# Attention's products with the values as three rounded passes, and the compressed branch as one pass over stacked rows

## The chip, the cores and the metric

The kernel runs on one core of one Trainium2 chip. The metric is the time of the program on the device in microseconds (us), as the median of several runs. TensorE (PE) does the matmuls, VectorE (DVE), ScalarE (ACT) and GpSimd (POOL) the rest, and SyncE (SP) issues the loads. Each of these engines takes its own instructions in turn, and semaphores make one wait for another.

## The reference

One decoder layer: a half-step SwiGLU block, a mixing block with sparse attention and retention side by side, an output projection, and a second half-step SwiGLU block, over 256 positions of width 2048 in float32. What the change touches is the attention, 16 heads of 128 in four groups that share keys and values. Each group has three branches, whose outputs are weighted by gates and added:

```
p_c = masked_softmax(s_c, mask)            # compressed: 15 keys, one per window of 32 positions
o_cmp = einsum('bghsc,bgcd->bsghd', p_c, v_cmp)
o_slc = einsum('bghqnr,bgqnrd->bqghd', p, vg)      # selected blocks (here: all of them)
o_win = einsum('bghnqk,bnkgd->bnqghd', p_w, vw)    # sliding window (here: all of it)
o = gates[:, :, 0] * o_cmp + gates[:, :, 1] * o_slc + gates[:, :, 2] * o_win
```

With 256 positions the selected and the window branch both reduce to causal attention over all keys, each with keys and values of its own.

## The kernel before

**Weights.** Nearly all time goes to products of activations with weights. The weights stream from memory in pieces of 256 rows by 512 columns. `prep` splits each piece (`split`, L134 to L136): ACT rounds it to fp32r (`whi`, L135) and DVE takes the rest (`wlo`, L136). `unit` (L210 to L217) then does one piece as 12 matmuls of 512 columns: high by high, high by low, low by high. One such piece is called a slot here. Up to four pieces are prepared ahead (`PREP`, `AHEAD`). The moving operand of these matmuls is read "by turns" (`by_turns`): one element of the first half, one of the second, and so on; `halves` undoes that where the result is read.

**Order.** The program fixes the order of every engine's instructions by hand (`manual_schedule`). Work that isn't a weight product is cut into small steps that wait in a list (`micro`). `run` takes the weight pieces in order and, after each one, takes one step from the list, so that a step's instructions stand on each engine between those of two slots. Within a step they are issued in the order in which its functions are called.

**Attention.** `attention(g)` projects keys and values of group g (8 slots, `kv_done` at the end), then queries (8 slots, `q_done` at the end). `q_done` adds the group's steps to the list; they are taken one by one during the next 16 slots, under the next group's projections. With the first counted as step 0, the steps are: `k_tr`, two empty ones, `q_tr`, `c_scores` (compressed branch), `scores(1, 1)`, and so on to step 8, `scores(1, 0)` with `scores(0, 0)`, which is taken behind the slot that ends the next group's keys and values and so behind its `kv_done`. Steps 9 to 14 are

```
both(p_tr(1, 1), softmax(1, 0), softmax(0, 0)), p_tr(0, 1), both(pv(1, (1,), False), c_tr),
both(pv(1, (0,), True), p_tr(1, 0), p_tr(0, 0)), None, pv(0, (1, 0), True)]
```

The arguments are branch and half of the queries (`pv`: half, branches, whether the compressed branch is added). `softmax` takes exponentials on ACT (L1004, four of them, each with a sum that is read out), makes weights of the sums on DVE (L931, L932) and POOL, and scales on POOL. `p_tr` transposes the probabilities on PE (L1016), 128 keys at a time, and copies them out of the bank on ACT (first 128 keys, L1021) or DVE (second, L1019). `pv` multiplies values and transposed probabilities in plain float32 (L1033), adds the compressed branch (L1037, 15 rows), and rounds and splits the sum on ACT and DVE (L1044, L1045). `c_tr` transposes the compressed branch's probabilities, 8 blocks of 15 columns (L973), and copies them on ACT (L974).

**Beginning of the mixing block.** `norm` prepares the first half of the positions (`at_once`), the first two slots run on it, and `head` then prepares the second half: DVE scales (L491), ACT rounds (L494), DVE takes the rest (L497). `mix` is the list of all items of the mixing block.

Of the kernel before, what the change touches and what calls it, by code (L numbers as in the profile page):

```python
# [72 lines left out]
def block_kernel(ctx: ExitStack, tc: tile.TileContext, I, konst, decay, out):  # L73
# [714 lines left out]
        return o  # L788

    kcT = cp.tile([P, GROUPS * NCMP], F32, name="kcT")  # L790
    vc = cp.tile([P, GROUPS, DH], F32, name="vc")

    def compress(i):
        def done(ps):
            z = evac(ps)
            box = {}

            def tr():
                zT = t4([P, 4, S])
                banks = to_banks(lambda t, k: z[:, t, k * P:(k + 1) * P])  # L800
                for b in range(2):
                    nc.vector.tensor_copy(zT[:, 2 * b:2 * b + 2], banks[b])
                zp = []
                for h in range(2):
                    zz = t4([P, GROUPS, NCMP, 16])
                    src = bass.AP(tensor=zT.tensor, offset=zT.offset + 16 * h,
                                  ap=[list(zT.ap[0]), [S, GROUPS], [16, NCMP], [1, 16]])
                    pb = pos[:, i, 16 * h:16 * h + 16][:, None, None, :].to_broadcast([P, GROUPS, NCMP, 16])
                    nc.vector.tensor_tensor(zz, src, pb, op=ALU.add)
                    zp.append(zz)  # L810
                box["zp"] = zp

            def first_layer(b):
                def f():
                    if b == 0:
                        box["ps"] = mx()
                    for jj in range(8):
                        j = 8 * b + jj
                        nc.tensor.matmul(box["ps"][:, :60], w1[i][b][:, jj, :],
                                         box["zp"][j // 16][:, :, :, j % 16], start=j == 0, stop=j == 31)  # L820
                    if b == 3:
                        g = small(60, "g60")
                        nc.scalar.activation(g, box["ps"][:, :60], AF.Gelu_apprx_tanh, bias=b1[:, i:i + 1])
                        box["g"] = g
                return f

            def second_layer():
                g = box["g"]
                ps2 = mx()
                if i == 1:  # L830
                    for k in range(GROUPS):
                        nc.tensor.matmul(ps2[0:NCMP, k * DH:(k + 1) * DH], g[:, k * NCMP:(k + 1) * NCMP],
                                         w2[:, 1, :], start=True, stop=True)
                    nc.vector.tensor_copy(vc[0:NCMP], ps2[0:NCMP, :].rearrange("p (g d) -> p g d", g=GROUPS))
                    return
                nc.tensor.matmul(ps2[0:60, :DH], g, w2[:, 0, :], start=True, stop=True)
                kn = t2([P, DH])
                junk = t2([P, DH])
                sc = small(1, "s1")
# [12 lines left out]
            push(tr, None, *[first_layer(b) for b in range(4)], None, second_layer)  # L852
            if i == 0:
                push(None, to_kcT)
        return done

    def gate_logits(hi, lo):
# [14 lines left out]
            nc.vector.tensor_copy(gates, ps[:, :96].rearrange("p (t c) -> p t c", t=2))  # L872
        push(tr)

    mix += in_chunk(O_KV, NCH, compress(0), head)
    mix += in_chunk(O_KV + NCH, NCH, compress(1))
    mix.append(("w", rows(win, 0, KT, O_GL, 48), KT, 48, gate_logits))
# [12 lines left out]
    def attention(g):  # L890
# [1 line left out]
        B3 = [P, 4, DH]  # L892

        def kv_done(ps):
            kv = evac(ps)
            box["kv"] = kv
            for t in range(2):
                ks = [kv[:, t, s * DH:(s + 1) * DH] for s in (0, 2)]
                sc = normed(ks, 2)
                for i, k in enumerate(ks):  # L900
                    nc.gpsimd.tensor_scalar(k, k, sc[:, i:i + 1], None, op0=ALU.mult)

        def q_done(ps):
            q = evac(ps)
# [4 lines left out]
            push(*steps)  # L909

        def k_tr():
            kv = box["kv"]
            kT = t2([P, 2, S])
            ps = mx([P, 2, S])
            for i in range(2):
                for t in range(2):
                    nc.tensor.transpose(ps[:, i, t * P:(t + 1) * P], kv[:, t, 2 * i * DH:(2 * i + 1) * DH], ident)
            for i in range(2):
                nc.scalar.activation(kT[:, i], ps[:, i], AF.Copy, scale=g_qk[:, 2 + i:3 + i])
            box["kT"] = kT  # L920
# [14 lines left out]
        def c_scores():  # L935
            qT = box["qT"]
            ps = mx()
            for t in range(2):
                for h in range(4):
                    c0 = (t * 4 + h) * NCMP  # L940
                    nc.tensor.matmul(ps[:, c0:c0 + NCMP], qT[:, h, t * P:(t + 1) * P],
                                     kcT[:, g * NCMP:(g + 1) * NCMP], start=True, stop=True)
            n = 8 * NCMP
            pc = small(n, "pc")
            pv = pc.rearrange("p (t h c) -> p t h c", t=2, h=4)
            p3 = pc.rearrange("p (a c) -> p a c", c=NCMP)
            nc.vector.tensor_tensor(pv, ps[:, :n].rearrange("p (t h c) -> p t h c", t=2, h=4),
                                    bias_c[:, :, 4 * g:4 * g + 4, :], op=ALU.add)
            m = small(8, "m8")
            nc.vector.tensor_reduce(m, p3, axis=AX.X, op=ALU.max)  # L950
            nc.vector.tensor_tensor(p3, p3, m[:, :, None].to_broadcast([P, 8, NCMP]), op=ALU.subtract)
            box["pc"] = pc

        def c_softmax():
# [9 lines left out]
            weigh(p3, sv, gates[:, :, 4 * g:4 * g + 4], 8)  # L964
            nc.gpsimd.tensor_tensor(p3, p3, s8[:, :, None].to_broadcast([P, 8, NCMP]), op=ALU.mult)

        def c_tr():
            pT = t4([P, 2, NCH])
            for t in range(2):
                ps = mx()  # L970
                for h in range(4):
                    c0 = (t * 4 + h) * NCMP
                    nc.tensor.transpose(ps[0:NCMP, h * P:(h + 1) * P], box["pc"][:, c0:c0 + NCMP], ident)  # L973
                nc.scalar.activation(pT[0:NCMP, t], ps[0:NCMP], AF.Copy)  # L974
            box["pcT"] = pT

        def scores(br, t):
# [32 lines left out]
        def p_tr(br, t):  # L1010
            def f():
                s = box["p", br, t]
                for j in range(t + 1):
                    ps = mx([P, 4, P])
                    for h in range(4):
                        nc.tensor.transpose(ps[:, h], s[:, h, j * P:(j + 1) * P], ident)  # L1016
                    pT = t2([P, 4, P])
                    if j:
                        nc.vector.tensor_copy(pT, ps)  # L1019
                    else:  # L1020
                        nc.scalar.activation(pT, ps, AF.Copy)  # L1021
                    box["pT", br, t, j] = pT
            return f

        def pv(t, brs, cmp_):
            def f():
# [3 lines left out]
                ps = box["o", t]  # L1030
                for br in brs:
                    for j in range(t + 1):
                        nc.tensor.matmul(ps, box["kv"][:, j, (2 * br + 1) * DH:(2 * br + 2) * DH],  # L1033
                                         box["pT", br, t, j].rearrange("p h q -> p (h q)"), start=start, stop=False)
                        start = False
                if cmp_:
                    nc.tensor.matmul(ps, vc[0:NCMP, g, :], box["pcT"][0:NCMP, t], start=False, stop=True)  # L1037
                    if t:
                        o_hi.append(act_hi())
                        o_lo.append(act_lo())  # L1040
                    hi = o_hi[g][:, :, t * P:(t + 1) * P]
                    lo = o_lo[g][:, :, t * P:(t + 1) * P]
                    pq = ps.rearrange("p (h q) -> p h q", h=4)
                    nc.scalar.activation(hi, pq, AF.Copy)  # L1044
                    nc.vector.tensor_tensor(lo, pq, hi.bitcast(F32), op=ALU.subtract)  # L1045
            return f
# [1 line left out]
        def both(*fns):  # L1048
            return lambda: [f() for f in fns]
        steps = [k_tr, None, None, q_tr, c_scores, scores(1, 1), both(softmax(1, 1), scores(0, 1)),  # L1050
                 both(softmax(0, 1), c_softmax), both(scores(1, 0), scores(0, 0)),
                 both(p_tr(1, 1), softmax(1, 0), softmax(0, 0)), p_tr(0, 1), both(pv(1, (1,), False), c_tr),
                 both(pv(1, (0,), True), p_tr(1, 0), p_tr(0, 0)), None, pv(0, (1, 0), True)]
        return (seg_chunk(O_KV + 1024, NCH, 4, g, DH, kv_done)
                + in_chunk(g * NCH, NCH, q_done))
# [193 lines left out]
```

## Time and profile before

| | before |
|---|---|
| median of 3 runs | 2503.43 us (2503.11 to 2505.05) |
| the profiled execution | 2505.49 us, of which its span is 2503.7 us |
| PE busy | 2445.5 us (98%) |
| DVE, ACT, POOL busy | 1737.4 us (69%), 1140.9 us (46%), 233.5 us (9%) |
| the four groups' attention steps | from 890 to 1131 us |

The page of the profile counts an engine busy while it executes an instruction. The timeline lists instructions by engine with start and length. PE's matmuls overlap in it, so that what one costs is the distance between two starts, not its listed length. A float32 matmul shows as two instructions. An idle time and what ended it stand in brackets behind a row.

### The profile page before, as it was taken

The page shows a single profiled execution, that of the slowest core. Times are in us where ns is not written, and L with a number is a line of the kernel's source. Part 1 is how long each engine was busy: PE and PEld are TensorE (multiplying, and loading weights), DVE is VectorE, ACT ScalarE, POOL GpSimd, SP SyncE. Part 2 cuts the span into 40 slices and gives each one's busy share as a digit, 9 for nine tenths or more (in the row PEclk, how much of TensorE's full clock was granted, in tenths as well). Part 3 has the DMA queues.
Part 4 walks back from the last instruction along what each step waited for, and adds up shares of the span by engine and source line. Part 5 has one row for each costly group of instructions (what it writes and reads, how often), then busy time and mean ns, then how long its engine had stood idle before and what let it go on. Part 6 is the DMA issues. An engine that isn't in the chain of part 4 may idle for free. (4 is left out here: it accounts for less than half of the span.)

```text
span 2503.7 us, 31546 instructions
## 1 busy us (share of the span) xinstructions
PE 2445.5 (98%) x11616; PEld 2120.0 (85%) x11616; DVE 1737.4 (69%) x1968; ACT 1140.9 (46%) x1416; POOL 233.5 (9%) x201
## 2 busy tenths in 40 slices
PE   4999999999999999999999999999999999999999
PEld 4888888888887888888888888888788888888888
DVE  7898777898756466776767777776688555555555
ACT  3545444444445355554444444444544444444443
POOL 0000000110002133320000000001100010001001
PEclk9999999999999999999999999999999999999999
DMA  9998888899866455667888877887499666666664
GB/s 347 350 321 277 280 301 293 305 311 344 280 222 196 140 158 143 185 195 261 280 264 262 256 246 235 294 273 250 153 320 352 198 203 199 200 199 203 200 202 153
DMA packets 348339, 616.64 MB, mean 246 GB/s; under 512 B 22044, under 2 KB 80018, under 8 KB 347928
## 3 DMA queue, kind: packets, MB, share of 16 engines
q1 hardware_dynamic: 348184, 614.63, 74.8%
q8 instruction: 91, 1.49, 0.2%
q14 instruction: 64, 0.52, 0.1%
HBM read 612.45 MB, written 2.10 MB: 245 GB/s over the span
## 5 line engine op out<-in xcount | busy, mean ns | idle before, releaser
L136 DVE TENSOR_TENSOR wlo<-raw,whi 128x1024 fp32r<-128x1024 f32 (+1 forms) x865 | 1082.1, 1260 | 575.4 <-ACT whi L135 570.4
L135 ACT ACTIVATE whi<-raw 128x1024 fp32r<-128x1024 f32 (+1 forms) x865 | 906.9, 1056 | 1002.2 <-PE accb L217 730.6
L215 PE MATMUL accb<-whi,ahi 128*128 128x512 f32 x3232 | 1240.5, 384 | 6.1 <-ACT ahi L494 4.7
L216 PE MATMUL accb<-wlo,ahi 128*128 128x512 f32 x3232 | 1229.4, 380 | 3.8 <-DVE wlo L136 3.5
L217 PE MATMUL accb<-whi,alo 128*128 128x512 f32 x3232 | 1228.4, 380 | 2.9 <-DVE alo L541 1.5
L215 PEld LDWEIGHTS accb<-whi,ahi 128*128 128x128 f32 x3232 | 612.8, 190 | 95.1 <-ACT ahi L494 5.5
L216 PEld LDWEIGHTS accb<-wlo,ahi 128*128 128x128 f32 x3232 | 613.0, 190 | 92.2 <-DVE wlo L136 8.0
L217 PEld LDWEIGHTS accb<-whi,alo 128*128 128x128 f32 x3232 | 612.7, 190 | 92.5 <-DVE alo L541 1.9
L344 DVE SCALAR_TENSOR_TENSOR aacc<-raw,cond,aacc 128x1024 f32<-128x1024 f32 x270 | 354.2, 1312 | 1.3 <-DMA raw<-in_w_ada_dram 0.6
L558 POOL TENSOR_TENSOR x<-x,t 128x512 f32<-128x512 f32 x50 | 80.9, 1639 | 1156.2 <-DVE t L556 989.0
L621 PE MATMUL accb<-wlo,ahi 128*128 128x512 f32 x224 | 87.1, 389 | 2.5 <-DVE wlo L136 2.5
L620 PE MATMUL accb<-whi,ahi 128*128 128x512 f32 x224 | 86.7, 387 | 0.0
L622 PE MATMUL accb<-whi,alo 128*128 128x512 f32 x224 | 85.9, 384 | 0.0
L621 PEld LDWEIGHTS accb<-wlo,ahi 128*128 128x128 f32 x224 | 43.0, 192 | 12.1 <-DVE wlo L136 6.2
L540 ACT ACTIVATE ahi<-mx 128x512 fp32r<-128x512 f32 x52 | 28.1, 593 | 53.9 <-PE mx L449 53.9
L541 DVE TENSOR_TENSOR alo<-mx,ahi 128x512 fp32r<-128x512 f32 x52 | 33.4, 684 | 27.2 <-ACT ahi L540 27.2
L620 PEld LDWEIGHTS accb<-whi,ahi 128*128 128x128 f32 x224 | 43.1, 192 | 6.1
L622 PEld LDWEIGHTS accb<-whi,alo 128*128 128x128 f32 x224 | 43.0, 192 | 6.0
L556 DVE TENSOR_TENSOR t<-accb,gt 128x512 f32<-128x512 f32 x56 | 36.3, 683 | 7.7 <-PE accb L217 7.6
L787 ACT ACTIVATE t<-accb 128x512 f32<-128x512 f32 x52 | 30.1, 593 | 24.2 <-PE accb L217 24.1
L1004 ACT ACTIVATE t<-t,m 128x256 f32<-128x256 f32 (+1 forms) x64 | 28.3, 443 | 26.0 <-DVE m L994 26.0
L1113 POOL TENSOR_SCALAR rs<-bmv 128x2 f32<-128x2 f32 x8 | 1.8, 220 | 395.3 <-DVE bmv L1112 395.2
(182 smaller groups left out, 1025.6 us busy)
## 6 DMA issues: line engine op xcount, KB each, us to landing
raw<-in_w_ada_dram SPq DMA_DIRECT2D x288, 512.0 KB, 5.5
raw<-in_w_ffn_gate_dram SPq DMA_DIRECT2D x176, 512.0 KB, 5.1
raw<-in_w_ffn_up_dram SPq DMA_DIRECT2D x176, 512.0 KB, 4.7
raw<-in_w_ffn_down_dram SPq DMA_DIRECT2D x176, 512.0 KB, 4.2
raw<-in_w_in_dram SPq DMA_DIRECT2D x176, 512.0 KB, 4.5
raw<-in_w_in_dram SPq DMA_DIRECT2D x128, 256.0 KB, 3.9
raw<-in_w_proj_nsa_dram SPq DMA_DIRECT2D x32, 512.0 KB, 5.7
raw<-in_w_proj_ret_dram SPq DMA_DIRECT2D x32, 512.0 KB, 5.4
```

What stands on the lines that cost most here:

```text
L135: nc.scalar.activation(hi_ap, raw_ap, AF.Copy)
L136: nc.vector.tensor_tensor(lo_ap, raw_ap, hi_ap.bitcast(F32), op=ALU.subtract)
L215: nc.tensor.matmul(ps[t], xh, wh, start=kt == 0, stop=False)
L216: nc.tensor.matmul(ps[t], xh, wl, start=False, stop=False)
L217: nc.tensor.matmul(ps[t], xl, wh, start=False, stop=kt == K - 1)
L344: nc.vector.scalar_tensor_tensor(box[0], raw, k, box[0], op0=ALU.mult, op1=ALU.add)
L541: nc.vector.tensor_tensor(lo[:, 2 * b:2 * b + 2], ps, h.bitcast(F32), op=ALU.subtract)
L556: nc.vector.tensor_tensor(in_two(y), halves(ps[t]), in_two(gt[:, n * NCH:(n + 1) * NCH]), op=ALU.mult)
L558: (nc.vector if last and n == 3 else nc.gpsimd).tensor_tensor(xs, xs, y, op=ALU.add)
L620: nc.tensor.matmul(ps, xh, h, start=i == 0, stop=False)
L621: nc.tensor.matmul(ps, xh, l, start=False, stop=False)
L622: nc.tensor.matmul(ps, xl, h, start=False, stop=i == nk - 1)
```

## The change

Values and transposed probabilities are now each split into a rounded high part and a low rest, as weights are, and each product is made of three fp32r passes, read by turns. `kv_done` writes keys and values to tiles of their own, the values in two parts. `p_tr` makes both parts of every bank (ACT the high one, DVE the low one). For the compressed branch the probabilities' high part, again the high part and the low part stand at columns 0, 32 and 64 of a zeroed tile `pc3`, and the values' high, low and high part at the same rows of `vc`, so that one fp32r pass over 79 rows gives the three products; a new function `c_split` fills `pc3`, and `clear` zeroes both tiles at the beginning of the mixing block. The list of steps is reordered and has 16 entries. The reading of the result undoes the turns.

```diff
+    CMP = 64 + NCMP
+    vc = cp.tile([P, GROUPS, DH], F32R, name="vc")
+    pc3 = cp.tile([P, 8, CMP], F32R, name="pc3")
+    def clear():
+        nc.scalar.activation(vc, ones[:, None, :].to_broadcast([P, GROUPS, DH]), AF.Copy, scale=0.0)
+        nc.scalar.activation(pc3, ones[:, None, :CMP].to_broadcast([P, 8, CMP]), AF.Copy, scale=0.0)
...
-                    nc.vector.tensor_copy(vc[0:NCMP], ps2[0:NCMP, :].rearrange("p (g d) -> p g d", g=GROUPS))
+                    v = ps2[0:NCMP, :].rearrange("p (g d) -> p g d", g=GROUPS)
+                    for r in (0, 64):
+                        nc.scalar.activation(vc[r:r + NCMP], v, AF.Copy)
+                    nc.vector.tensor_tensor(vc[32:32 + NCMP], v, vc[0:NCMP].bitcast(F32), op=ALU.subtract)
...
+    mix.append(("do", clear))
     mix += in_chunk(O_KV, NCH, compress(0), head)
...
         def kv_done(ps):
-            kv = evac(ps)
-            box["kv"] = kv
+            k = t2([P, 2, 2, DH])
+            v = t4([P, 2, 2, 2, DH], F32R)
+            box["k"], box["v"] = k, v
             for t in range(2):
-                ks = [kv[:, t, s * DH:(s + 1) * DH] for s in (0, 2)]
+                kv = halves(ps[t])
+                nc.scalar.activation(k[:, t], kv[:, :, :DH], AF.Copy)
+                nc.scalar.activation(v[:, 0, t], kv[:, :, DH:], AF.Copy)
+                nc.vector.tensor_tensor(v[:, 1, t], kv[:, :, DH:], v[:, 0, t].bitcast(F32), op=ALU.subtract)
+            for t in range(2):
+                ks = [k[:, t, i] for i in range(2)]
...
+        def c_split():
+            p3 = box["pc"].rearrange("p (a c) -> p a c", c=NCMP)
+            for c in (0, 32):
+                nc.scalar.activation(pc3[:, :, c:c + NCMP], p3, AF.Copy)
+            nc.vector.tensor_tensor(pc3[:, :, 64:CMP], p3, pc3[:, :, :NCMP].bitcast(F32), op=ALU.subtract)
+
         def c_tr():
-            pT = t4([P, 2, NCH])
+            pT = t4([P, 2, NCH], F32R)
...
-                    nc.tensor.transpose(ps[0:NCMP, h * P:(h + 1) * P], box["pc"][:, c0:c0 + NCMP], ident)
-                nc.scalar.activation(pT[0:NCMP, t], ps[0:NCMP], AF.Copy)
+                    nc.tensor.transpose(ps[0:CMP, h * P:(h + 1) * P], pc3[:, t * 4 + h].bitcast(F32), ident)
+                nc.scalar.activation(pT[0:CMP, t], ps[0:CMP], AF.Copy)
...
-                    pT = t2([P, 4, P])
-                    if j:
-                        nc.vector.tensor_copy(pT, ps)
-                    else:
-                        nc.scalar.activation(pT, ps, AF.Copy)
-                    box["pT", br, t, j] = pT
+                    hi = t2([P, NCH], F32R)
+                    lo = t2([P, NCH], F32R)
+                    pf = ps.rearrange("p h q -> p (h q)")
+                    nc.scalar.activation(hi, pf, AF.Copy)
+                    nc.vector.tensor_tensor(lo, pf, hi.bitcast(F32), op=ALU.subtract)
+                    box["pT", br, t, j] = by_turns(hi), by_turns(lo)
...
-                        nc.tensor.matmul(ps, box["kv"][:, j, (2 * br + 1) * DH:(2 * br + 2) * DH],
-                                         box["pT", br, t, j].rearrange("p h q -> p (h q)"), start=start, stop=False)
+                        ph, pl = box["pT", br, t, j]
+                        vh, vl = box["v"][:, 0, j, br], box["v"][:, 1, j, br]
+                        nc.tensor.matmul(ps, vh, ph, start=start, stop=False)
+                        nc.tensor.matmul(ps, vh, pl, start=False, stop=False)
+                        nc.tensor.matmul(ps, vl, ph, start=False, stop=False)
...
-                    nc.tensor.matmul(ps, vc[0:NCMP, g, :], box["pcT"][0:NCMP, t], start=False, stop=True)
+                    nc.tensor.matmul(ps, vc[0:CMP, g, :], by_turns(box["pcT"][0:CMP, t]), start=False, stop=True)
...
-                 both(p_tr(1, 1), softmax(1, 0), softmax(0, 0)), p_tr(0, 1), both(pv(1, (1,), False), c_tr),
+                 both(p_tr(1, 1), softmax(1, 0), softmax(0, 0), c_split), c_tr, both(pv(1, (1,), False), p_tr(0, 1)), None,
                  both(pv(1, (0,), True), p_tr(1, 0), p_tr(0, 0)), None, pv(0, (1, 0), True)]
```

## Rows read from the trace of the kernel before

**Rows 1.** The page, busy time: engine, busy us (share of span), instructions.
```profile
PE 2445.5 (98%) x11616; PEld 2120.0 (85%) x11616; DVE 1737.4 (69%) x1968; ACT 1140.9 (46%) x1416; POOL 233.5 (9%) x201
```
**Rows 2.** Busy time by stretch, second group's later steps: span, engines (instructions), clock, DMA.
```profile
990.00:1010.00 20.00, 20.00 (x83) 13.52 (x82) 11.97 (x16) 9.60 (x14) 5.86 (x6) 1.00 0.74 211
```
**Rows 3.** Groups of PE's instructions by form: busy us, mean ns, idle before.
```profile
L1033 PE MATMUL mx<-t,t 128*128 128x512 f32 x48 | 22.6, 592 | 0.0
...
L1037 PE MATMUL mx<-t,vc 15*128 15x512 f32 x16 | 9.0, 640 | 0.0
```
**Rows 4.** Timeline of PE, second group's steps 11 and 12: start, length, instruction.
```profile
989.89 1.88 PE L1033 MATMUL mx<-t,t 128*128 128x512 f32 x4
991.61 1.04 PE L973 MATMUL mx<-kc,pc 128*15 128x128 f32 x8
...
992.70 0.38 PE L216 MATMUL accb<-wlo,ahi 128*128 128x512 f32 x1
...
995.07 1.88 PE L1033 MATMUL mx<-t,t 128*128 128x512 f32 x4
996.88 1.12 PE L1037 MATMUL mx<-t,vc 15*128 15x512 f32 x2
997.93 1.09 PE L1016 MATMUL mx<-kc,t 128*128 128x128 f32 x8
```
**Rows 5.** Timeline of PE, gate logits: fp32r passes read straight, 256 columns.
```profile
833.34 0.28 PE L862 MATMUL mx<-ahi,whi 128*48 128x256 f32 x1
...
833.69 0.28 PE L862 MATMUL mx<-ahi,whi 128*48 128x256 f32 x1
```
**Rows 6.** Timeline of PE and ACT, second group: transposes of step 10, exponentials of step 9.
```profile
986.42 1.04 PE L1016 MATMUL mx<-kc,t 128*128 128x128 f32 x8
...
986.56 0.40 ACT L1004 ACTIVATE t<-t,m 128x128 f32<-128x128 f32 x1 [2.37 <-DVE m L994]
...
989.32 0.38 ACT L1004 ACTIVATE t<-t,m 128x128 f32<-128x128 f32 x1
...
990.65 0.57 ACT L1021 ACTIVATE t<-mx 128x512 f32<-128x512 f32 x1
```
**Rows 7.** Timeline of DVE, second group, step 9 and the split behind it.
```profile
989.87 0.68 DVE L1019 COPY t<-mx 128x512 f32<-128x512 f32 x1
990.47 0.22 DVE L931 TENSOR_SCALAR s<-s 128x4 f32<-128x4 f32 x1
...
991.09 1.24 DVE L136 TENSOR_TENSOR wlo<-raw,whi 128x1024 fp32r<-128x1024 f32 x1
```
**Rows 8.** Timeline, the same places in the first and in the fourth group.
```profile
925.54 1.04 PE L1016 MATMUL mx<-kc,t 128*128 128x128 f32 x8
...
928.01 0.68 DVE L1019 COPY t<-mx 128x512 f32<-128x512 f32 x1
...
1108.82 1.04 PE L1016 MATMUL mx<-kc,t 128*128 128x128 f32 x8
...
1112.92 0.39 ACT L1004 ACTIVATE t<-t,m 128x128 f32<-128x128 f32 x1
```
**Rows 9.** Groups of DVE's instructions by form, from 790 to 1135 us.
```profile
L1045 DVE TENSOR_TENSOR alo<-mx,ahi 128x512 fp32r<-128x512 f32 x8 | 5.5, 691 | 23.6 <-ACT ahi L1044 23.6
...
L962 DVE TENSOR_REDUCE s<-pc 128x8 f32<-128x120 f32 x4 | 1.1, 278 | 11.5 <-POOL pc L960 11.5
```
**Rows 10.** Timeline of DVE and PE at the beginning of the mixing block.
```profile
779.11 1.22 DVE L136 TENSOR_TENSOR wlo<-raw,whi 128x1024 fp32r<-128x1024 f32 x1
780.24 0.74 DVE L491 TENSOR_TENSOR t<-t,mx 128x256 f32<-128x256 f32 x2
...
781.15 0.64 PE L215 MATMUL accb<-whi,ahi 128*128 128x512 f32 x1 [1.41 <-ACT ahi L494]
```
**Rows 11.** PE by stretch, around 491 us: span, busy (instructions), granted clock, DMA.
```profile
489.00:491.00 2.00, 0.53 (x3) 1.00 1.06 393
491.00:494.40 3.40, 3.40 (x9) 0.53 0.91 320
```

More of the change, by code (lines that the diff above doesn't have):

```diff
@@ L790, in block_kernel @@
     kcT = cp.tile([P, GROUPS * NCMP], F32, name="kcT")
-    vc = cp.tile([P, GROUPS, DH], F32, name="vc")
+    CMP = 64 + NCMP
[4 more added lines that the diff above has]
+        nc.scalar.activation(pc3, ones[:, None, :CMP].to_broadcast([P, 8, CMP]), AF.Copy, scale=0.0)
     def compress(i):
@@ L894, in kv_done @@
         def kv_done(ps):
-            kv = evac(ps)
-            box["kv"] = kv
+            k = t2([P, 2, 2, DH])
+            v = t4([P, 2, 2, 2, DH], F32R)
+            box["k"], box["v"] = k, v
             for t in range(2):
-                ks = [kv[:, t, s * DH:(s + 1) * DH] for s in (0, 2)]
+                kv = halves(ps[t])
[4 more added lines that the diff above has]
+                ks = [k[:, t, i] for i in range(2)]
                 sc = normed(ks, 2)
-                for i, k in enumerate(ks):
-                    nc.gpsimd.tensor_scalar(k, k, sc[:, i:i + 1], None, op0=ALU.mult)
+                for i, kk in enumerate(ks):
+                    nc.gpsimd.tensor_scalar(kk, kk, sc[:, i:i + 1], None, op0=ALU.mult)
         def q_done(ps):
@@ L911, in k_tr @@
         def k_tr():
-            kv = box["kv"]
+            k = box["k"]
             kT = t2([P, 2, S])
@@ L916, in k_tr @@
                 for t in range(2):
-                    nc.tensor.transpose(ps[:, i, t * P:(t + 1) * P], kv[:, t, 2 * i * DH:(2 * i + 1) * DH], ident)
+                    nc.tensor.transpose(ps[:, i, t * P:(t + 1) * P], k[:, t, i], ident)
             for i in range(2):
@@ L943, in c_scores @@
             n = 8 * NCMP
-            pc = small(n, "pc")
+            pc = sp.tile([P, n], F32, tag="pc", name="pc", bufs=2)
             pv = pc.rearrange("p (t h c) -> p t h c", t=2, h=4)
@@ L971, in c_tr @@
                 for h in range(4):
-                    c0 = (t * 4 + h) * NCMP
-                    nc.tensor.transpose(ps[0:NCMP, h * P:(h + 1) * P], box["pc"][:, c0:c0 + NCMP], ident)
-                nc.scalar.activation(pT[0:NCMP, t], ps[0:NCMP], AF.Copy)
+                    nc.tensor.transpose(ps[0:CMP, h * P:(h + 1) * P], pc3[:, t * 4 + h].bitcast(F32), ident)
+                nc.scalar.activation(pT[0:CMP, t], ps[0:CMP], AF.Copy)
             box["pcT"] = pT
@@ L1042, in f @@
                     lo = o_lo[g][:, :, t * P:(t + 1) * P]
-                    pq = ps.rearrange("p (h q) -> p h q", h=4)
+                    pq = ps.rearrange("p (k q a) -> p a k q", a=2, k=2)
+                    hi, lo = (z.rearrange("p (a k) q -> p a k q", a=2) for z in (hi, lo))
                     nc.scalar.activation(hi, pq, AF.Copy)
```

## The prediction, as it was put on record

> **What bounds the kernel now.** I read the page's busy times first: PE is busy for 98% of the span [rows 1]. In the attention stage it is busy without a break, 20.00 of 20.00 us at the full granted clock, with DVE at 60% and ACT at 48% [rows 2]. The list of PE's waits has no entry for it there. So each microsecond taken from PE's list is a microsecond of the whole, and so is each microsecond for which PE has to stand; DVE and ACT have room, and what they add costs nothing unless PE meets it before it is done. The timeline then gives prices (PE by the distance of starts, since its lengths overlap) and, what decides here, the order: which instruction stands behind which on ACT and DVE at the moment when PE comes to ask for the result.
>
> **What PE saves.** Of float32 products with the values there are 24 in the kernel, recorded as 48 instructions, and 8 of the compressed branch, recorded as 16 [rows 3]. Two products of the first kind last from 989.89 to 991.61, 1.72 us, and 1.81 us where a compressed one follows (995.07 to 996.88); that one lasts from 996.88 to 997.93, 1.05 us [rows 4]. A group has three such pairs (1.72 + 1.81 + 1.81 = 5.34 us) and two compressed products (2.10 us). An fp32r pass of 512 columns by turns costs 0.2155 us: eleven from 992.70 to 995.07 [rows 4]. Afterwards a group has 18 passes (3.88 us) and 2 (0.43 us). It saves 5.34 - 3.88 = 1.46 us and 2.10 - 0.43 = 1.67 us, together 3.13 us, and four groups **12.5 us**. The number of transposes stays; those of the compressed branch get 79 columns for 15, which I count as nothing, since the 128-column ones show the same length (1.04 us for eight, [rows 4, 6]).
>
> These passes read their moving operand by turns. In this trace that costs nothing: 0.2155 us for 512 columns is 0.42 ns each [rows 4], while three straight ones of 256 columns take 0.35 us, 0.46 ns each [rows 5]. The Trainium skill, page "Advanced Engine Details and Errata", section "SBUF Cachelines", says the opposite: an access that lands on a different line each time pays a penalty. It gives no figure. It appears as a rival below.
>
> **What ACT and DVE get.** Per group, DVE makes six low parts where it made two copies, two low parts of the values (128x256 each) and one of the compressed probabilities; ACT makes six high parts for four and some small copies. A low part of 128x512 is priced by the existing one, 0.69 us alone [rows 9], and 0.60 us from start to start, as the copy of this size (989.87 to 990.47, [rows 7]). The two of 128x256 cost 0.72 us, by a pair of that size that reads a bank (0.74, [rows 10]). The small one of 128x120 costs 0.28, by the reduction over as much [rows 9]. That is 2.40 + 0.72 + 0.28 = 3.4 us of DVE more per group of some 60 us, on an engine with 40% free in the stage where most of it falls [rows 2]. As a sum it is hidden.
>
> **Where it is not hidden.** Step 9 now ends with `c_split`, and step 10, one slot later, is `c_tr`, which needs its result. In the second group PE comes to step 10 at 986.42. At 986.56 ACT only begins step 9's eight exponentials, because DVE has their maxima no earlier; the last starts at 989.32 and takes 0.38 [rows 6]. `c_split`'s copies are called after them. That ACT doesn't go past an instruction that waits can be seen in the same rows: PE has finished step 10's transposes before 987.5, and their copy runs at 990.65, behind the exponentials and a weight split. Before the change nothing on PE needed these copies until two slots later. Afterwards PE stands.
>
> For how long? On DVE the chain is longer than on ACT. The first instruction of step 9 stood at 989.87 [rows 7]. It is put back by the two low parts of the values, 0.72, which stand in `kv_done` on the same busy stretch. Then two low parts of the probabilities run for one copy, 1.20; then the sums' block, 0.62 (990.47 to 991.09, [rows 7]); then the small low part, 0.28; and 0.15 to get PE started. That makes 989.87 + 2.97 = 992.84, and PE has stood for 992.84 - 986.42 = 6.4 us. In the first group the start is 928.01 and PE's turn 925.54 [rows 8]: 930.98, or 5.4 us. The third group's rows repeat the first's with 0.2 us more, 5.6 us. The fourth has no `kv_done` behind it, but its exponentials end late, at 1113.3 [rows 8]; the second sums' block (here 0.75 with its start) and 0.43 give 1114.5 against 1108.82, or 5.7 us. In all **23.1 us**. Below it is bounded by ACT's queue alone: the last exponential's end, then a copy and the low part (0.28 each, [rows 9]) and the start, 0.71 in all, which is 3.8, 4.0, 4.0 and 5.2 us, or 17 us. Above it is bounded by DVE's lengths without overlap, 0.69 for every low part, those of the values too: 25.8 us. PE can't make it up: it is busy without a break afterwards.
>
> Queued behind `c_split` are, on DVE and ACT, the weight splits of the slot four places on. They have three slots of some 2.6 us in hand, so no second wait. The later hand-overs (`p_tr` to `pv`) keep two slots' distance, over 5 us, for some 2 us of copying; they cost nothing, and without that cover would cost up to the 0.6 us of a low part.
>
> **PE's clock.** Around 491 us PE was busy for 0.53 of 2.00 us, and the next nine matmuls ran at a mean granted clock of 0.53, that is nearly all at 1.2 instead of 2.4 GHz: 3.40 us [rows 11] instead of 9 x 0.2155 = 1.94. The new pauses are longer than that one. I count one such loss, 1.46 us, behind each, **5.8 us**; the bounds are none and twice as much.
>
> **At the beginning of the block** `clear` puts two copies of 512 and 632 elements on ACT in front of a weight split. By an ACT copy of 512 elements, 0.57 us [rows 6], they take 0.57 x 1144 / 512 = 1.27, less a little overlap: **1.2 us**. DVE's half of that split (779.11) stands before the scaling (780.24) for which PE in the end waits 1.41 us [rows 10], so the delay reaches PE whole; below, it is nothing if DVE finds another order of work, above 1.5. Making `vc` in three instructions for one is nothing: no step needs it for dozens of slots.
>
> **Sum.** Against the profiled execution, 2505.5 (span 2503.7 and 1.8 around it): 2505.5 - 12.5 + 23.1 + 5.8 + 1.2 = 2523.1. The median of the runs is 2.1 lower, so I predict 2521.0 us, slower by 0.7%. Without any wait it would be 2492.
>
> **Rivals.**
> - *The split is ready in time* (the other side, faster). The place is step 10, and it decides at 2.8 us per group: PE saves 12.5, `clear` takes 1.2 back, and 11.3 over four is what each wait may cost. It would need the exponentials to start over 3 us earlier, or the copies to get in front of them. For it speaks that the compressed probabilities themselves are ready early, since they are softmaxed two steps before. Against it, ACT's queue alone gives 3.8 us in the group where it is shortest. Without a wait: 2492. Chance 0.07. With waits of some 2.5 us and no loss of clock, 2502: 0.04.
> - *The wait is there, the clock doesn't fall.* For it speaks that one place is no rule; against it, [rows 11]. 2515. Chance 0.16.
> - *The passes don't run at the price of the existing ones* (the change doesn't do what it says). If each cost 0.43 us, half of a float32 product [rows 4], 80 passes would add 17 us: 2538. That is the direction of the skill's rule on lines; [rows 4, 5] contradict it. Chance 0.03.
> - *DVE falls behind for longer*, so that further hand-overs wait: 2530 to 2540. Chance 0.05.
>
> My own case has 0.65. Its terms taken low (saving 13.1 with breaks like the 0.09 us between 1.72 and 1.81 that go too, waits 18.5, clock 2.9, `clear` 1) give 2512.7, taken high (25.8, 10 and 1.5 against 12) 2528.7; with the case without the fall of clock the range is 2511 to 2529. A difference under 0.2%, 5 us, can hardly be told from no change here. Faster by more than that: 0.07, the case without a wait. Within it: 0.05, from the shorter waits and the lowest of the others. Slower: 0.88.
>
> **What will show it.** Right: before `c_tr`'s transposes PE idles 5 to 6.5 us in each of the four groups, ended by the low part of `pc3` on DVE; a stretch of half clock follows; a pair of products takes 1.3 us and the compressed pass 0.22; the 1.41 us wait at the beginning of the mixing block [rows 10] grows to 2.6 us. Wrong: PE without a break from 890 to 1120 us; or `c_split`'s copies ahead of the exponentials on ACT; or passes of more than 0.22 us. If the waits are there but are ended by ACT, the DVE part of my chain is too long.

## The result and the profile after

The changed kernel takes 2522.52 us in the median of 4 runs (2520.75 to 2523.82) against 2503.36 (2503.11 to 2505.05), a ratio of 1.0077, with a 95% interval from 1.0062 to 1.0091: 0.77% slower, 19.2 us. (One run of `cmp_alone` below, 4186 us at a mean granted clock of 0.58 where the others have 0.99, belongs to a slow state and is left out of its figures.) The profiled execution took 2523.82 us, its span 2522.0 us against 2503.7, which is 18.3 us longer.

The page of after, busy times as in [rows 1]:

```profile
PE 2442.0 (97%) x11632; PEld 2133.0 (85%) x11632; DVE 1746.1 (69%) x1996; ACT 1149.8 (46%) x1444; POOL 237.0 (9%) x201
```

PE is busy for 3.5 us less, while the span grew by 18.3. PE's list of waits from 885 to 1160 us, which holds the four groups and had no entry in the kernel before, says where it stands (engine, line waited at, what ended it: us in total, times, longest):

```profile
PE mx L996 <- DVE pc L989: 11.7, 2, 5.9
PE mx L996 <- ACT whi L135: 10.1, 2, 5.1
PE mx L449 <- POOL t L925: 3.1, 2, 1.6
```

L996 are `c_tr`'s transposes: four waits, 21.8 us. The list counts a wait from the end of the matmul before it, which is modelled, and leaves out idle times of little more than 0.1 us; from the moment at which the next pass would have started, each wait is 0.16 us longer. L449 are the next group's transposes of queries: 3.1 us, and no part of the prediction. The timeline of the second group shows the first kind, to be laid beside [rows 6, 7]:

```profile
990.08 0.38 ACT L1027 ACTIVATE t<-t,m 128x128 f32<-128x128 f32 x1
...
990.47 0.48 ACT L988 ACTIVATE pc<-pc 128x120 fp32r<-128x120 f32 x2
...
990.63 1.27 DVE L1044 TENSOR_TENSOR t<-mx,t 128x512 fp32r<-128x512 f32 x2
991.83 0.15 DVE L949 TENSOR_SCALAR s<-s 128x4 f32<-128x4 f32 x1
...
992.38 0.25 DVE L989 TENSOR_TENSOR pc<-pc,pc 128x120 fp32r<-128x120 f32 x1
...
992.78 1.97 PE L996 MATMUL mx<-kc,pc 128*79 128x128 f32 x8 [5.84 <-DVE pc L989]
```

`c_split`'s two copies (L988) stand on ACT behind the last exponential; on DVE its low part (L989) stands behind the two low parts of the probabilities (L1044) and the sums' block (L949 and on). PE starts at 992.78. In two groups the list names ACT's weight split as what ended the wait, since that event was the last by the profile; PE has nothing to do with it there, and L989 has just ended in these groups too (in the first at 926.04, and PE starts at 926.19).

The eight transposes take 1.97 us where they took 1.04 [rows 4], and what follows is slow as well: from 925 to 932 us nearly all of it runs at 1.2 instead of 2.4 GHz. The same view of PE by stretch as [rows 11] (span, busy time with instructions, granted clock, DMA), once for 230 us of the four groups' steps and once for two of the pauses:

```profile
915.00:1145.00 230.00, 205.09 (x1025) 0.94 0.52 155
...
925.00:932.00 7.00, 5.81 (x18) 0.52 0.55 150
990.00:1000.00 10.00, 7.22 (x30) 0.66 0.67 191
```

The products themselves do what was said of them; the timeline of PE, second group, as [rows 4]:

```profile
998.35 0.38 PE L1058 MATMUL mx<-t,t 128*128 128x512 f32 x1
998.57 0.38 PE L1059 MATMUL mx<-t,t 128*128 128x512 f32 x1
...
999.43 0.38 PE L1060 MATMUL mx<-t,t 128*128 128x512 f32 x1
999.65 1.04 PE L1039 MATMUL mx<-kc,t 128*128 128x128 f32 x8
...
1014.57 0.38 PE L1063 MATMUL mx<-t,vc 79*128 79x512 f32 x1
1014.79 0.38 PE L215 MATMUL accb<-whi,ahi 128*128 128x512 f32 x1
```

Six passes take from 998.35 to 999.65, 1.30 us instead of 1.72. The compressed branch's pass starts at 1014.57 and the next one at 1014.79: 0.22 instead of 1.05.

**Where the 18.3 us arise.** Every weight pass (L215 to L217) stands in both traces, so one can ask at each of them how far the changed kernel is behind. Ahead of the mixing block, at 770 us, it is 5.3 us early; at 885 us, ahead of the attention, 4.5 us early; behind the attention 18.6 us late; at the end 18.3. So the attention costs **23.1 us**, and the beginning of the mixing block, where `clear` stands, 0.8. The 5.3 us are no part of the change. Stretches at half clock fall elsewhere in this execution (that of [rows 11] isn't there at all), which makes 1.9 us near 150 us and 1.6 near 491, and a wait near 490 us is 0.8 us shorter; all of this lies in parts of the kernel that the change doesn't touch.

Inside the attention the 23.1 us are made up as follows. The instructions of steps 10 to 15, at full clock and with their waits taken out, last 6.96 us a group where they lasted 10.23, so 13.1 us are saved. The waits before `c_tr` are 22.4 us beyond PE's turn. The clock costs about 10.6 (experiment 3), and the queries wait 2.9 us more than before. 22.4 + 10.6 + 2.9 - 13.1 = 22.8.

### The profile page after: what moved, and what is told of

It reads as the page before. It is cut to its first block, busy times and chain, and to the rows that moved or that the text cites. A ratio compares the mean times of both kernels' runs of the same rounds, so it can differ in the third digit from the quotient of the medians.

```text
span 2522.0 us, 31643 instructions
## 1 busy us (share of the span) xinstructions
PE 2442.0 (97%) x11632; PEld 2133.0 (85%) x11632; DVE 1746.1 (69%) x1996; ACT 1149.8 (46%) x1444; POOL 237.0 (9%) x201
## 5 line engine op out<-in xcount | busy, mean ns | idle before, releaser
L136 DVE TENSOR_TENSOR wlo<-raw,whi 128x1024 fp32r<-128x1024 f32 (+1 forms) x865 | 1077.2, 1255 | 574.4 <-ACT whi L135 568.8
L215 PE MATMUL accb<-whi,ahi 128*128 128x512 f32 x3232 | 1243.9, 385 | 7.1 <-ACT ahi L494 5.7
L216 PE MATMUL accb<-wlo,ahi 128*128 128x512 f32 x3232 | 1232.2, 381 | 1.4 <-DVE wlo L136 0.9
L217 PE MATMUL accb<-whi,alo 128*128 128x512 f32 x3232 | 1231.4, 381 | 2.1 <-DVE alo L724 0.9
L215 PEld LDWEIGHTS accb<-whi,ahi 128*128 128x128 f32 x3232 | 615.4, 190 | 94.0 <-ACT ahi L494 6.5
L217 PEld LDWEIGHTS accb<-whi,alo 128*128 128x128 f32 x3232 | 614.4, 190 | 92.0 <-DVE alo L724 1.6
L216 PEld LDWEIGHTS accb<-wlo,ahi 128*128 128x128 f32 x3232 | 615.2, 190 | 90.4 <-DVE wlo L136 5.2
L621 PEld LDWEIGHTS accb<-wlo,ahi 128*128 128x128 f32 x224 | 42.8, 191 | 10.6 <-DVE wlo L136 4.4
```

Of the source, the lines that this page charges most:

```text
L136: nc.vector.tensor_tensor(lo_ap, raw_ap, hi_ap.bitcast(F32), op=ALU.subtract)
L215: nc.tensor.matmul(ps[t], xh, wh, start=kt == 0, stop=False)
L216: nc.tensor.matmul(ps[t], xh, wl, start=False, stop=False)
L217: nc.tensor.matmul(ps[t], xl, wh, start=False, stop=kt == K - 1)
L621: nc.tensor.matmul(ps, xh, l, start=False, stop=False)
```

## The experiments

**My theory:** the passes are a gain; the loss is the order of steps 9 and 10, which makes PE meet `c_split` some 6 us too early, and the fall of the clock that follows each pause. **Rivals:** the three-pass products or their low parts on DVE are themselves the loss; the copies' place on ACT is what matters, not the distance; the clock costs little. All kernels but two are made from the changed one. The place of `c_tr` is a matter of the list of steps; steps 9 to 12 of it are, in the changed kernel:

```
both(p_tr(1, 1), softmax(1, 0), softmax(0, 0), c_split), c_tr, both(pv(1, (1,), False), p_tr(0, 1)), None,
```

**1. `c_tr` two steps later** (`ctr_at_12`)

```diff
-                 both(p_tr(1, 1), softmax(1, 0), softmax(0, 0), c_split), c_tr, both(pv(1, (1,), False), p_tr(0, 1)), None,
+                 both(p_tr(1, 1), softmax(1, 0), softmax(0, 0), c_split), None, both(pv(1, (1,), False), p_tr(0, 1)), c_tr,
```

> The changed kernel with one edit: the transposes of the compressed branch stand at step 12 instead of step 10, which is left empty. If the cost is one of order (PE meets the split of the compressed probabilities three microseconds after it was called), the four waits of 5.1 to 6.0 us before these transposes go. A smaller wait takes their place at step 11, since PE now comes to the first products with the values some 7 us earlier and the low parts are late on DVE: 2.1 us in the second group, 0.5 to 1.3 in the others, about 5 in all, with little or no half clock behind: 2499 us, 2495 to 2506. If the cost is the added DVE and ACT work as such, the waits move and keep their sum of 22 us: 2518 to 2524.

Measured: 2496.86 us, 0.9970 of before (0.9960 to 0.9981). PE's waits in the stage, and PE's line over the same 230 us as above:

```profile
PE mx L1059 <- DVE t L1044: 3.5, 4, 1.6
PE mx L449 <- POOL t L925: 3.1, 2, 1.6
```

```profile
915.00:1145.00 230.00, 223.39 (x1165) 1.00 0.61 185
```

The wait at `c_tr` is gone and the clock is full. Two positions in a list are worth 25.7 us, and turn a loss of 0.77% into a gain of 0.3%. What is late next shows as well: no pause stands ahead of `pv(1, (1,))` any more, and at its second pass (L1059) the low part of the probabilities isn't there. The prediction had called this hand-over free; it was so only behind the pause.

**2. The split called first in its step** (`split_first`)

```diff
-                 both(p_tr(1, 1), softmax(1, 0), softmax(0, 0), c_split), c_tr, ...
+                 both(c_split, p_tr(1, 1), softmax(1, 0), softmax(0, 0)), c_tr, ...
```

> The changed kernel with one edit: in step 9 the split of the compressed probabilities is called first, before the transposes and the exponentials. If DVE's queue sets the end of the wait, as I worked it out, DVE comes to step 9 late anyway and PE still waits 3 to 4.6 us per group, 15 us in all instead of 22: about 2514 us. If ACT's exponentials set it, the copies now run before them and the waits shrink to under 1 us: about 2495.

Measured: 2510.5 us, 1.0030 (1.0018 to 1.0041). The wait, and the timeline of the second group:

```profile
PE mx L996 <- DVE pc L989: 13.4, 4, 4.1
```

```profile
985.86 0.69 DVE L1017 TENSOR_REDUCE m<-t 128x4 f32<-128x512 f32 x1
986.47 1.22 DVE L136 TENSOR_TENSOR wlo<-raw,whi 128x1024 fp32r<-128x1024 f32 x1
987.60 0.86 DVE L342 TENSOR_SCALAR aacc<-raw,cond 128x1024 f32<-128x1024 f32 x1
988.38 0.27 DVE L989 TENSOR_TENSOR pc<-pc,pc 128x120 fp32r<-128x120 f32 x1
988.57 1.27 DVE L1044 TENSOR_TENSOR t<-mx,t 128x512 fp32r<-128x512 f32 x2
...
988.80 1.07 PE L996 MATMUL mx<-kc,pc 128*79 128x128 f32 x8 [4.11 <-DVE pc L989]
```

Now the copies are ahead of the exponentials on ACT and the low part ahead of the probabilities' on DVE, and PE still stands for 4.11 us. PE's turn was at 984.69 (988.80 - 4.11). What remains is DVE's own lateness: until 986.5 it is still at work on the step before (L1017, the maxima), and then on a weight slot (L136, L342). The place within the step is worth 21.8 - 13.4 = 8.4 us of waiting, and the rest went only when the distance grew (experiment 1). So it was DVE's queue that set the end of these waits, as the prediction's chain had it, and ACT's alone was not the point.

**3. The pause filled with work** (`filled`). It adds passes whose bank nobody reads.

```diff
         def c_tr():
+            idle = mx()
+            for _ in range(22):
+                nc.tensor.matmul(idle, box["v"][:, 0, 0, 1], box["pT", 1, 1, 0][0], start=True, stop=True)
```

> The changed kernel with 22 fp32r passes added per group in front of the transposes of the compressed branch, into a bank that nobody reads: 4.7 us of PE work inside the wait of 5.1 to 6.0 us. If the pause itself brings the granted clock down, the half clock behind the waits goes and with it 2.7 us per group, 11 in all, although PE has more to do: about 2511 us, waits of 0.4 to 1.3 us left. If the clock falls for another reason (the transposes, say), the half clock stays: 2520 to 2524.

Measured: 2514.01 us, 1.0039 (1.0026 to 1.0053). PE's waits, and PE by stretch:

```profile
PE mx L449 <- POOL t L925: 3.1, 2, 1.6
PE mx L999 <- DVE pc L989: 2.2, 2, 1.1
PE mx L999 <- ACT whi L135: 0.6, 2, 0.4
```

```profile
915.00:1145.00 230.00, 224.04 (x1169) 1.00 0.54 163
```

88 passes of 0.2155 us are 19.0 us, and 2.8 us of waiting remain: together 21.8, exactly the idle time that they replace. So PE is no earlier at `c_tr`, and everything that this kernel gains is the clock: 0.94 becomes 1.00, the attention costs 12.5 us where it cost 23.1, **10.6 us** less, some 2.6 us for each pause. Work that nobody needs makes this kernel 8.5 us faster.

**4. One slot more** (`seventeen`): the list with 17 steps, `pv(1, (1,))` at step 12 and `c_tr` at step 13.

```diff
+                 both(p_tr(1, 1), softmax(1, 0), softmax(0, 0), c_split), None, None, both(pv(1, (1,), False), p_tr(0, 1)), c_tr,
```

> The changed kernel with 17 steps per group: after step 9 two empty steps, then the first products with the values, then the transposes of the compressed branch, and the rest behind. If only the order was wrong, all waits of the later steps are gone and the gain of PE is left: 13.1 us less 0.5 for the zeroing and up to 3 for the queries' transposes, 2491 to 2494 us. If the added work on DVE is what costs, 2510 or more.

Measured: 2496.0 us, 0.9975 (0.9965 to 0.9985). Both waits of experiment 1 are gone, and another has come:

```profile
PE accb L216 <- DVE wlo L136: 5.3, 5, 2.0
```

It isn't better than experiment 1. A weight slot now waits for its own low part: DVE, with the same work, meets PE at another place. The steps also slide: a group has 16 slots, so with 17 steps each group's `k_tr` comes 17 slots behind the last one's, and the waits stand in the second and third group alone. My number for it was too low for this reason. The profile is of an execution of 2501.28 us, well above the median, so its waits need not be those of the other runs.

**5. The values' products alone** (`pv_alone`): made from the kernel before, with the values and probabilities split and multiplied in three passes, and the compressed branch in plain float32 as before, without `clear` and `c_split`. Steps 9 to 12 have the changed kernel's order.

```diff
-                 both(p_tr(1, 1), softmax(1, 0), softmax(0, 0)), p_tr(0, 1), both(pv(1, (1,), False), c_tr),
+                 both(p_tr(1, 1), softmax(1, 0), softmax(0, 0)), c_tr, both(pv(1, (1,), False), p_tr(0, 1)), None,
```

> One part of the change alone: the products with the values in three passes, the compressed branch in float32 as before (no zeroing, no split of its probabilities, its transposes at step 10). If the waits come from the split of the compressed probabilities, PE doesn't wait at step 10; it saves some 6 us, pays 3 to 4 at step 11 for the low parts and 3 at the queries' transposes: within 3 us of the kernel before, 2501 to 2506. If the added low parts on DVE are the cause, the waits of the whole change are here too: 2515 or more.

Measured: 2502.13 us, 0.9998 (0.9989 to 1.0008), and hardly any wait:

```profile
PE mx L1047 <- DVE t L1032: 0.8, 1, 0.8
PE mx L449 <- POOL t L918: 0.7, 2, 0.3
```

The rival that the three passes, or their low parts on DVE, are themselves the loss falls. But the gain is small too: the attention is 1.4 us shorter where three pairs a group save 4 x 1.46 = 5.8. One reason is that both branches are added in one bank, so that the compressed float32 product had to be read by turns here, which the expectation had not thought of. The timeline (to be laid beside [rows 4]):

```profile
995.71 0.38 PE L1046 MATMUL mx<-t,t 128*128 128x512 f32 x1
...
997.09 1.34 PE L1051 MATMUL mx<-t,vc 15*128 15x512 f32 x2
998.36 1.09 PE L1027 MATMUL mx<-kc,t 128*128 128x128 f32 x8
```

It takes 1.27 us, where the same product read straight took 1.05: eight times 0.22 are 1.8 us. The six passes ahead of it take 1.38 us (995.71 to 997.09) and not 1.30, which makes 0.6 more in eight places. With 1.5 us of waits that leaves 1.9 of the 5.8, near the 1.4 measured.

**6. The stacked branch alone** (`cmp_alone`): made from the kernel before, with `pc3`, `clear` and `c_split`, in the changed order of steps; the values' products in plain float32, again read by turns.

```diff
-                 both(p_tr(1, 1), softmax(1, 0), softmax(0, 0)), p_tr(0, 1), both(pv(1, (1,), False), c_tr),
+                 both(p_tr(1, 1), softmax(1, 0), softmax(0, 0), c_split), c_tr, both(pv(1, (1,), False), p_tr(0, 1)), None,
```

> The other part alone: the compressed branch in one stacked pass, the products with the values in float32 as before (copies by ACT and DVE as before, no low parts). If the split of the compressed probabilities causes the waits, they stay, shorter by the low parts that DVE no longer makes ahead of it: 4.1, 5.1, 4.3 and 5.7 us, 19 in all, with most of the half clock behind, against 7 us saved: about 2524 us, 2518 to 2528. If the low parts are the cause, the waits go and 2497 is left.

Measured: 2527.77 us in the median of three runs, 1.0100 (1.0084 to 1.0115). Waits and PE's timeline:

```profile
PE mx L990 <- DVE pc L983: 18.2, 4, 5.5
PE mx L449 <- POOL t L919: 3.1, 2, 1.6
```

```profile
998.13 2.33 PE L1051 MATMUL mx<-t,t 128*128 128x512 f32 x4
1000.29 1.04 PE L1033 MATMUL mx<-kc,t 128*128 128x128 f32 x8
```

The waits are back, on average 0.9 us shorter in a group than with the values' low parts. The two experiments together put the loss on `c_split` with its place. The attention's 27.8 us are 18.2 and 2.9 of waits, less 6.7 for the compressed products, plus 5.3 for the float32 products by turns (two take 998.13 to 1000.29, 2.16 us instead of 1.72, so 24 x 0.22), and 8.1 that remain for the clock, over four pauses. PE worked for 17.1 us at half clock there, half of which is 8.5.

**7. `pv(0)` back at step 14** (`pv0_at_14`): experiment 1, and the last product one slot earlier, as in the kernel before.

```diff
-                 both(pv(1, (0,), True), p_tr(1, 0), p_tr(0, 0)), None, pv(0, (1, 0), True)]
+                 both(pv(1, (0,), True), p_tr(1, 0), p_tr(0, 0)), pv(0, (1, 0), True)]
```

> The kernel with the compressed transposes at step 12, and one more edit: the last products with the values at step 14 instead of 15, as they stood before the change. The low part of the result then leaves DVE one slot ahead of the sums of squares of the queries. If that low part is what makes the queries late, PE's wait for their scaling by POOL falls from 1.6 us in two groups to 0.3: 2494 us against 2497. If the wait is POOL's alone (its scaling takes 2.9 us where it took 1.9), it stays: 2497.

Measured: 2493.09 us, 0.9962 (0.9948 to 0.9976). The queries' wait for POOL is gone (its scaling in the third group takes 1.90 us again); only that at L1059 stays:

```profile
PE mx L1059 <- DVE t L1044: 3.5, 4, 1.6
```

**8. All of it together** (`best1`): experiment 7, with the passes on the low probabilities last, so that PE asks for DVE's part at the fifth pass instead of the second, and `clear` 40 items earlier, away from the beginning of the mixing block.

```diff
+    items.insert(len(items) - 40, ("do", lambda: clear()))
...
-    mix.append(("do", clear))
...
+                        ph = box["pT", br, t, j][0]
+                        for i in range(2):
+                            nc.tensor.matmul(ps, box["v"][:, i, j, br], ph, start=start, stop=False)
+                            start = False
+                for br in brs:
+                    for j in range(t + 1):
+                        nc.tensor.matmul(ps, box["v"][:, 0, j, br], box["pT", br, t, j][1], start=False, stop=False)
```

> The kernel with the compressed transposes at step 12 and the last products at 14, and two more edits: the passes of a pair are ordered so that those with the low part of the probabilities come last, and the zeroing stands some 40 items earlier. The four waits at step 11 shrink from 3.5 to about 1 us in all, and the second wait at the beginning of the mixing block falls back from 2.1 to 1.4: about 2491 us. If PE is held there by DVE for longer than four passes, only the 2494 of the kernel without these two edits is left.

Measured: 2490.94 us, 0.9952 (0.9939 to 0.9964), with one kind of wait left in the list, and PE's timeline at that place in the second group:

```profile
PE mx L1062 <- DVE t L1044: 1.2, 2, 1.0
```

```profile
979.82 1.03 PE L1058 MATMUL mx<-t,t 128*128 128x512 f32 x4
981.83 1.08 PE L1062 MATMUL mx<-t,t 128*128 128x512 f32 x2 [0.97 <-DVE t L1044]
982.74 1.04 PE L1039 MATMUL mx<-kc,t 128*128 128x128 f32 x8
```

The list shows only part of it. From the first pass to the transposes it is 2.92 us here, where six passes without a wait take 1.30: 1.62 us of waiting, since each of the two passes on a low part is late. Read so, step 11 still waits for 3.5 us in the four groups, against some 4.5 in experiments 1 and 7. The order of the passes is therefore worth 1.0 us, less than expected. The zeroing costs nothing at its new place: by the weight passes the kernel is 6.6 us early at 770 us and 6.7 at 885.

This beats both kernels: it is 0.48% faster than before, where the changed one is 0.77% slower. It is about the time that the prediction gave for the change without any wait, 2492; since waits of 3.5 us remain, part of that agreement is luck.

The attention's cost by the weight passes, beside the sum of what each trace shows (saving 13.1; waits as listed; the queries' wait less the 0.2 us that it lasted before; the added passes):

| kernel | saving, waits, added | sum | measured | left over |
|---|---|---|---|---|
| changed | -13.1 + 21.8 + 2.9 | 11.6 | 23.1 | 11.5 |
| `filled` | -13.1 + 2.8 + 2.9 + 19.0 | 11.6 | 12.5 | 0.9 |
| `split_first` | -13.1 + 13.4 + 2.9 | 3.2 | 9.1 | 5.9 |
| `ctr_at_12` | -13.1 + 3.5 + 2.9 | -6.7 | -5.6 | 1.1 |
| `seventeen` | -13.1 + 5.3 - 0.2 | -8.0 | -5.0 | 3.0 |
| `pv0_at_14` | -13.1 + 3.5 | -9.6 | -8.5 | 1.1 |
| `best1` | -13.1 + 1.2 | -11.9 | -9.5 | 2.4 |

Where the clock stays full some 1 us is left over. That is no smaller saving, but the list's count: by the starts of the passes each of the four waits at step 11 is 0.26 us longer than listed in `ctr_at_12` and `pv0_at_14`, 1.0 us in all, and in `best1` they come to 3.5 us instead of 1.2, which is the 2.4 us of the last row but for 0.1. Where the clock falls, 10.6 us more is left over than in `filled`, and with shorter pauses (`split_first`) about half of that. In `seventeen` it falls too, from 994 to 997.5 us.

## Why the prediction was right, point by point

The forecast was 2521.0 us, 1.5 below the median measured, and its mechanism held in each group. Its terms:

- **The saving.** 12.5 us predicted, 13.1 measured. 13.1 is what the steps last less, and the table bears it out. Six passes took 1.30 us, the compressed one 0.22. The transposes of 79 columns cost nothing more, as counted: from start to start eight take 0.79 us in `ctr_at_12`, like those of 128. The rival by which the passes don't run at the price of the existing ones fell.
- **The waits before `c_tr`.** 23.1 us predicted, 22.4 measured beyond PE's turn: 5.1, 6.0, 5.2 and 6.0 us in the four groups, against 5.4, 6.4, 5.6 and 5.7. The chain on DVE was the right one, link by link. In the second group its first link (L1044) starts 3.85 us behind PE's turn, at 990.63, where the working had 4.17; from there PE starts 2.15 us later, where it had 2.25. So what stands ahead of step 9 put it back by less than the 0.72 us counted. (That PE was to start at 992.84 and started at 992.78 is chance: PE's turn came 0.36 us later in this trace.) ACT's queue alone, the lower bound of 17 us, did not set the end: there the copies had ended at 990.95, and the low part began at 992.38. With the split called first, ahead of the exponentials, 13.4 us were still left, all of them DVE's.
- **The clock.** This term was mis-sized: 5.8 us predicted, 10.6 shown by `filled`, near its upper bound (11.7). It was sized by a pause of 1.5 us, behind which half clock lasted for 3.40 us [rows 11]. Here it begins within each pause and lasts for 6.83 us; PE works for 6.0, 4.2, 5.8 and 5.7 us of it, with `c_tr`'s own transposes first, and half of these 21.7 us is 10.8. In `split_first`, with pauses of 4.1 us and less, there were three stretches of 3.4.
- **The queries' wait** is the step that was missing. POOL scales the next group's queries beside the last steps, and PE then transposes them. In the kernel before, POOL took 1.90 us and PE waited 0.26; now, in the third group and the fourth, it is this (timeline of after):

```profile
1024.29 1.22 DVE L136 TENSOR_TENSOR wlo<-raw,whi 128x1024 fp32r<-128x1024 f32 x1 [0.41 <-ACT whi L135]
...
1024.33 2.94 POOL L925 TENSOR_TENSOR t<-t,s 128x1024 f32<-128x1024 f32 x1
...
1027.33 1.09 PE L449 MATMUL mx<-kc,t 128*128 128x128 f32 x8 [1.57 <-POOL t L925]
```

  POOL's scaling starts 0.04 us behind a weight split on DVE and takes 2.94 us. Nothing in the change touches these instructions; it moved them against each other. "No second wait" looked at DVE and ACT and left out POOL, whose scaling there is on the path. It costs 2.9 us, some 2.1 by the longer scaling and the rest by its later start, and with `pv(0)` one step earlier (`pv0_at_14`) it is gone.
- **`clear`.** 1.2 us predicted, 0.8 measured at the block's beginning. The wait of 1.41 us [rows 10] did grow, to 2.2 (and not to 2.6), with a longer stretch at half clock (6.8 us instead of 3.4); but a wait of 1.0 us on a weight's low part (L216, in the list of waits of before a little later) then vanished. What a wait puts back it takes from the next one.
- **Outside the change** the profiled execution was 5.3 us early ahead of the mixing block, most of it by stretches of half clock that fall otherwise. So the number came out near the median partly because two things offset each other: the clock and the queries' wait cost 7.7 us more than the sum had, and 5.3 us came back from a place that it didn't look at, 0.7 from shorter waits, 0.4 from `clear` and 0.6 from the saving. That this comes so close is luck. The range, not the closeness, is what the working had earned.
- **The later hand-overs** cost nothing in the changed kernel, as predicted, but for a reason that the prediction didn't give: PE was late itself. Without the pause they cost 3.5 us by the list and 4.5 by the starts of the passes (`ctr_at_12`).

## What to carry to other kernels

Where the program fixes each engine's order, price a hand-over by the last instruction that stands ahead of the producer on its own engine when the consumer's turn comes, not by the producer's input or its length; here a 0.25 us instruction held PE for 6 us, and two positions in a list were worth 25.7 us. A pause of PE can be paid twice, once as idle time and once as slow passes behind it, so move the consumer back rather than the producer forward, and expect the next-latest hand-over to show up. And follow the moved work on every engine that carries one instruction of the path, also where that engine is busy for 9% of the span.

## What the runs showed of the hardware that I had not expected

**The clock around pauses.** In each of the changed kernel's four pauses of 5 to 6 us the granted clock fell to one half before PE had work again, and stayed there for 6.8 us in all, which cost some 2.6 us; with the pause filled it was 1.00 throughout. But the length of a pause doesn't tell how long half clock lasts. The same view by stretch, of the changed kernel's first pause and of the last one in `cmp_alone`, a wait of 5.5 us:

```profile
925.33:932.16 6.83, 5.97 (x18) 0.50 0.56 153
...
1130.66:1134.07 3.41, 2.98 (x11) 0.50 0.38 90
```

Behind 1.5 us it had been 3.40 us [rows 11], behind a wait of 3.35 us in the third group of `split_first` the clock didn't fall, and at the beginning of the changed kernel's mixing block half clock lasted for 6.8 us with no wait over 2.2 us. What sets the length stays open; what it costs is half of what PE works in it.

**DVE and POOL run some instructions one after the other.** The kernel before, timeline of DVE and POOL at the place of the three rows above:

```profile
1018.71 1.90 POOL L907 TENSOR_TENSOR t<-t,s 128x1024 f32<-128x1024 f32 x1
...
1019.10 2.59 DVE L136 TENSOR_TENSOR wlo<-raw,whi 128x1024 fp32r<-128x1024 f32 x1 [0.84 <-ACT whi L135]
```

Here POOL starts first, takes 1.90 us as in the first two groups, and DVE's split takes 2.59 instead of 1.22. In the changed kernel DVE starts first, by 0.04 us, and takes 1.22, and POOL takes 2.94. In both cases the later one ends about when the two in turn would: 1018.71 + 1.90 + 1.22 = 1021.83 against 1021.69, and 1024.29 + 1.22 + 1.90 = 1027.41 against 1027.27. The Trainium skill, page "SBUF — State Buffer", section "SBUF: two separate sides", says that a DVE instruction with two inputs in SBUF and a POOL instruction that reads SBUF share a pair of ports as a lock, which whoever comes first keeps for the whole instruction. These rows agree with it. The stretched row stood in the trace of before, on DVE, where it cost nothing.

**Reading by turns costs something in float32 and nothing in fp32r.** A float32 product of 512 columns took 1.08 us by turns (2.16 for two) and 0.86 straight, an fp32r pass 0.2155 us by turns (0.42 ns per column) against 0.46 ns per column straight, there at 256 columns [rows 5]. So the rule of the Trainium skill ("Advanced Engine Details and Errata", "SBUF Cachelines"), which these rows had contradicted for fp32r, has the right direction for float32; whether the lines are the cause wasn't tried. It means that mixing the two kinds in one bank has a price, which two of the experiments paid.
